# Three SwiGLUs of a decoder trunk: gate and up with the activations stationary and 512 weight columns moving, turned back by 32x32 blocks and on-chip transfers

## The chip, the cores and the metric

The kernel runs on one core of a Trainium2 chip. Its engines are TensorE (PE, matmuls; its weight loads are listed as PEld), VectorE (DVE), ScalarE (ACT), GpSimd (POOL) and the sync engine (SP), which here issues most transfers. The metric is device time in microseconds (us), the median of several runs. One execution is also taken by the hardware profiler; what is quoted as rows below comes from that one.

## The reference

A trunk of two layers over 256 tokens of width 1024, all in fp32. Each layer is a half-step SwiGLU, a token mixer (block-sparse attention in the first layer, latent attention in the second), and another half-step SwiGLU; each of these is preceded by an RMS norm and a shift and scale from the condition `c`, and added back with a gate from `c`. The part that the change touches:

```python
def swiglu(h, w_gate, w_up, w_down):      # D_MODEL = 1024, D_FF = 2816
    return (jax.nn.silu(h @ w_gate) * (h @ w_up)) @ w_down
```

There are four of these: two in each layer.

## The kernel before

**Precision.** Every fp32 operand is split into a high half and a low half in a 32-bit format that TensorE takes at full rate. ACT writes the high half (`hi`, L690) and DVE the low half (`lo`, L691). A product is three matmuls, high by high, high by low and low by high (`mm3`, L897 to L900).

**Weights.** They stream in the order in which they are used, 1 MB at a time, by SP's queue into `raw` (three buffers), and are split into `hi` and `lo` pieces of 128x1024 (eight buffers of each). A weight transfer (L838) waits until a `raw` buffer is free, which is when DVE's `lo` has read it.

**A SwiGLU.** Tokens are two tiles of 128 (`t`), the width 1024 is eight contraction tiles (`k`), and D_FF is 22 blocks of 128 (`f`). The first SwiGLU has a method of its own and is untouched. In the other three, the first four f-blocks (512 columns) are computed with `h` stationary and the weight columns moving: 48 matmuls of 512 columns per token tile, tokens on partitions. ACT takes the Silu (L1077), DVE the product (L1078), and PE turns the result by four 128x128 transposes (L1083) so that f lies on partitions, as the down projection needs it. The other 18 f-blocks are computed with a weight block stationary and `h` moving, so that f lies on partitions at once: for gate and up, eight matmuls of 512 columns (high and low half of `h` side by side, L1112) and eight of 256 (L1120). Here ACT copies one half of the sums (L1124), DVE adds the other (L1125); for every two f-blocks come one Silu (L1127), one product (L1128) and one split into `gh` and `gl` (L913, L914). These halves, called gT, are the stationary side of the down projection, in two halves of 512 output columns; its matmuls are the same `mm3`, with `gh` and `gl` in the place of `h`.

**Buffers.** The accumulators `mm` are a ring of four PSUM banks. `sums` is a pool with two buffers of each tile. `ry` has one buffer.

**Other work.** DVE also reduces the columns of the conditioning weights (`adaw`, L705 and L746) whenever there is room. For each sub-layer a row of gates is written to memory and read back over all partitions on POOL's queue (`gate_d<-grow`, L766, then `gate<-gate_d`, L754).

**Order.** The instructions are not run as written. A planner (`Order`) gives each instruction a cost (`duration`), simulates the engines, and fixes the order on every engine; a wait at the head of an engine's row holds what stands behind it.

Of the kernel before, what the change touches and what calls it, by code (L numbers as in the profile page):

```python
# [63 lines left out]
T_WAIT = 5.6  # L64
TQ_WAIT = 5.4
# [7 lines left out]
G_WAIT = 2.6  # L73
# [22 lines left out]
def weight_tiles():  # L96


    for layer in range(2):
        for idx in range(2):  # L100
            wg, wu, wd = (("ffn_w_" + n, (layer, idx)) for n in ("gate", "up", "down"))
            if (layer, idx) != (0, 0):
                for w in (wg, wu):
                    for k0 in range(0, KD, 4):
                        yield [(*w, 0)], k0, 4, FB
            for f0 in range(FB if (layer, idx) != (0, 0) else B1 * P, F, S):
                for w in (wg, wu):
                    yield [(*w, f0)], 0, KD, min(S, F - f0)
# [26 lines left out]
def lay_out(v):  # L135
# [8 lines left out]
    def rows(k0, j, cols, n, at, c, width=None, step=1, first=0):  # L144
        k = step * j + first if width else k0 + j
        return v[n][at][k * P:(k + 1) * P, c:c + (width or cols)]
# [73 lines left out]
def duration(i, aps):  # L220
# [19 lines left out]
    if e == "DVE":  # L240
# [5 lines left out]
        elif kind == "InstTensorCopy":  # L246
            d = 150.0 + (1.045 if psum else 0.53) * n
        elif kind == "InstMemset":
# [18 lines left out]
class Order:  # L267
# [128 lines left out]
    def place(self, need, nudge={}):  # L396
# [80 lines left out]
        while placed < n:  # L477
# [29 lines left out]
            if self.dma[k]:  # L507
# [3 lines left out]
                dur = dma_free + 850.0 - t  # L511
                if t < HELD and elements(self.aps[k][-1]) * self.aps[k][-1].ap[0][1] <= D:
                    dur = LONE
                if e != "Pool":
# [61 lines left out]
def trunk(ctx: ExitStack, tc: tile.TileContext, a: dict, out: bass.AP):  # L576
# [252 lines left out]
    def wload():  # L829
# [4 lines left out]
        widths = [p[3] for p in parts] if not cols else [cols * len(parts)]  # L834
# [200 lines left out]
    def ffn(layer, idx, h, after, ada_to, start=None, early=None):  # L1035

        last = (layer, idx) == (1, 1)
        with ExitStack() as st:
# [24 lines left out]
            accs = {t: [] for t in range(NT)}  # L1063
            parts = [[], []]
            for t in range(0 if start else NT):
                for i, pl in enumerate(parts):
                    ps = mm_tile()
                    for k in range(KD):
                        if len(pl) <= k:
                            pl += nextw()  # L1070
                        mm3(ps, *hk(h[t], k), *pl[k], start=k == 0, stop=k == KD - 1)
                        if last and not last_ffn:
                            last_ffn.append(nc.cur_bb.bb.instructions[-1].name)
                    accs[t].append(ps)
                acc = accs.pop(t)
                g = sumsp.tile([P, 1024], F32, tag="both", name=nm("g"))[:, :FB]
                nc.scalar.activation(g, acc[0], AF.Silu)  # L1077
# [864 lines left out]
```

## Time and profile before

| what | value |
|---|---|
| median of 3 runs | 976.93 us (976.6 to 978.33) |
| the profiled execution | 976.26 us |
| its span on the core | 974.0 us |
| instructions on PE, DVE, ACT, POOL | 5494, 1392, 1083, 136 |
| bytes moved | 268.29 MB, 275 GB/s |

The span is what the engine rows cover; the rest of the execution's time lies around it. Shares of busy time are averages over the whole program. A wait at one place is seen only in the stretch in which it lies.

### The profile page before, as it was taken

How to read it: one execution, taken by the hardware profiler on the slowest of the kernel's cores; microseconds unless marked ns; L12 is line 12 of the kernel's file. 1: busy time of each engine (PE TensorE's matmuls, PEld its weight loads, DVE VectorE, ACT ScalarE, POOL GpSimd, SP SyncE). 2: the span in 40 equal slices, each digit the busy share in tenths (PEclk: the TensorE clock that was granted, in tenths of full speed). 3: DMA queues.
4: the chain of work that ended last, by engine and by line, in shares of the span. 5: the costliest groups of instructions: out<-in, count | busy, mean ns of one | idle time of the engine just before them, and what ended most of it. 6: DMA issues, size and time to landing. Idle time of an engine off the chain costs nothing.

```text
span 974.0 us, 15044 instructions
## 1 busy us (share of the span) xinstructions
PE 966.2 (99%) x5494; PEld 827.3 (85%) x5494; DVE 828.5 (85%) x1392; ACT 594.1 (61%) x1083; POOL 87.4 (9%) x136
## 2 busy tenths in 40 slices
PE   8999999999999999999999999999999999999998
PEld 7998888888887888888888888888998888888887
DVE  7999999799999999998696699988998798566643
ACT  5689654378666956555377556543689595665521
POOL 2021100022130000000010000000143000000000
PEclk9999999999999999999999999999999999999999
DMA  9988889899877899999786599996553377545630
GB/s 357 408 345 286 323 321 365 302 356 344 322 272 248 291 352 347 328 335 335 280 318 244 203 313 360 349 393 218 196 167 118 131 261 277 197 173 195 237 130 22
DMA packets 56097, 268.29 MB, mean 275 GB/s; under 512 B 6734, under 2 KB 7960, under 8 KB 38104
## 3 DMA queue, kind: packets, MB, share of 16 engines
q1 hardware_dynamic: 53232, 259.23, 72.1%
q0 software_dynamic: 2352, 7.77, 2.6%
q8 instruction: 43, 0.70, 0.3%
q10 hardware_dynamic: 440, 0.34, 0.2%
q14 instruction: 30, 0.25, 0.1%
HBM read 263.09 MB, written 4.23 MB: 274 GB/s over the span
## 4 chain that ended last, share of the span: by engine, by line
PE 97%; DVE 2%; issue 0%; DMA 0%; POOL 0%; ACT 0%; DVEq 0%
PE mm L1112 25%; PE mm L898 16%; PE mm L900 16%; PE mm L899 16%; PE mm L1120 13%; PE at L1198 1%; PE at L1245 1%; PE at L1271 1%; PE tr L948 1%; DVE lo L691 1%; PE tr L1693 1%; PE mm L1884 1%; PE mm L1883 1%; PE mm L1885 1%; DVE adaw L705 1%; PE tr L1393 1%
## 5 line engine op out<-in xcount | busy, mean ns | idle before, releaser
L691 DVE TENSOR_TENSOR lo<-raw,hi 128x1024 fp32r<-128x1024 f32 (+2 forms) x302 | 360.1, 1212 | 78.7 <-ACT hi L690 69.2
L690 ACT ACTIVATE hi<-raw 128x1024 fp32r<-128x1024 f32 (+2 forms) x302 | 307.4, 1045 | 141.4 <-PE mm L900 98.8
L1112 PE MATMUL mm<-h,hi 128*128 128x512 f32 x1104 | 266.2, 392 | 1.3 <-DVE both L1125 1.1
L1112 PEld LDWEIGHTS mm<-h,hi 128*128 128x128 f32 x1104 | 202.3, 188 | 41.0 <-DVE both L1125 1.6
L1120 PEld LDWEIGHTS mm<-h,lo 128*128 128x128 f32 x1104 | 142.7, 191 | 5.8
L1120 PE MATMUL mm<-h,lo 128*128 128x256 f32 x1104 | 146.3, 283 | 0.0
L705 DVE CUSTOM_DVE_ANT_0 adaw<-adaw,c_b,cols 128x1024 f32<-128x1024 f32 (+1 forms) x112 | 140.0, 1268 | 2.1 <-DMA adaw<-in_ada_dram 2.1
L899 PE MATMUL mm<-lo,gh 128*128 128x512 f32 (+1 forms) x356 | 138.0, 388 | 0.0
L898 PE MATMUL mm<-hi,gh 128*128 128x512 f32 (+1 forms) x356 | 138.0, 388 | 0.0
L900 PE MATMUL mm<-hi,gl 128*128 128x512 f32 (+1 forms) x356 | 137.7, 387 | 0.0
L898 PE MATMUL mm<-hi,h 128*128 128x512 f32 (+2 forms) x256 | 99.3, 391 | 0.0
L899 PE MATMUL mm<-lo,h 128*128 128x512 f32 (+2 forms) x256 | 97.8, 385 | 0.0
L900 PE MATMUL mm<-hi,h 128*128 128x512 f32 (+2 forms) x256 | 97.6, 386 | 0.0
L900 PEld LDWEIGHTS mm<-hi,gl 128*128 128x128 f32 x356 | 66.9, 188 | 13.5
L899 PEld LDWEIGHTS mm<-lo,gh 128*128 128x128 f32 x356 | 66.9, 188 | 13.2
L898 PEld LDWEIGHTS mm<-hi,gh 128*128 128x128 f32 x356 | 66.8, 188 | 13.1
L1124 ACT ACTIVATE both<-mm 128x256 f32<-128x256 f32 x108 | 39.8, 376 | 39.6 <-PE mm L1120 38.2
L746 DVE CUSTOM_DVE_ANT_0 adaw<-adaw,c_b,cols 128x1024 f32<-128x1024 f32 x48 | 60.9, 1286 | 0.0
L898 PEld LDWEIGHTS mm<-hi,h 128*128 128x128 f32 x256 | 48.1, 188 | 9.2 <-issue 1.2
L900 PEld LDWEIGHTS mm<-hi,h 128*128 128x128 f32 x256 | 48.1, 188 | 9.1 <-DVE h L914 0.6
L899 PEld LDWEIGHTS mm<-lo,h 128*128 128x128 f32 x256 | 48.1, 188 | 7.8
L913 ACT ACTIVATE gh<-both 128x512 fp32r<-128x512 f32 x27 | 17.0, 631 | 60.8 <-DVE both L1128 60.8
(271 smaller groups left out, 1173.1 us busy)
## 6 DMA issues: line engine op xcount, KB each, us to landing
raw<-in_w_dram SPq DMA_DIRECT2D x140, 1024.0 KB, 6.1
adaw<-in_ada_dram SPq DMA_DIRECT2D x158, 512.0 KB, 6.0
raw<-in_w_dram SPq DMA_DIRECT2D x14, 512.0 KB, 4.1
raw<-in_first_dram SPq DMA_DIRECT2D x7, 512.0 KB, 9.8
raw<-in_first_dram SPq DMA_DIRECT2D x9, 384.0 KB, 9.6
gate<-gate_d POOLq DMA_DIRECT2D x6, 512.0 KB, 8.4
bg<-bias_d POOLq DMA_DIRECT2D x4, 768.0 KB, 6.5
adaw<-in_lat_dram SPq DMA_DIRECT2D x6, 512.0 KB, 6.6
```

Of the source, the lines that this page charges most:

```text
L690: nc.scalar.activation(hi, src, AF.Copy)
L691: nc.vector.tensor_tensor(lo, src, hi.bitcast(F32), op=ALU.subtract)
L705: nc.vector.tensor_tensor_reduce(wt[:, cs], wt[:, cs], c_b[:, cs], 1.0, at, op0=ALU.mult, op1=ALU.add, accum_out=m_cols[:, i, c:c + 1])
L746: nc.vector.tensor_tensor_reduce(wt, wt, c_b, 1.0, places["gates"][:, c:c + 1], op0=ALU.mult, op1=ALU.add, accum_out=g_cols[:, row, k:k + 1])
L898: nc.tensor.matmul(ps, lh, rh, start=start, stop=False)
L899: nc.tensor.matmul(ps, lh, rl, start=False, stop=False)
L900: nc.tensor.matmul(ps, ll, rh, start=False, stop=stop)
L913: nc.scalar.activation(hi, ps, AF.Copy)
L948: nc.tensor.transpose(kslice(pt, j), kslice(y, j), ident)
L1112: nc.tensor.matmul(ps, wh, hk_both(h, k).rearrange("p i t q -> p (i t q)"), start=k == 0, stop=False)
L1120: nc.tensor.matmul(ps[:, S:], wl, hk_both(h, k)[:, 0].rearrange("p t q -> p (t q)"), start=False, stop=k == KD - 1)
L1124: nc.scalar.activation(sums, ps[:, S:], AF.Copy)
```

## The change

In the second, third and fourth SwiGLU all of gate and up is computed with `h` stationary. D_FF is cut into five blocks of 512 and one of 256 columns; in the last one gate and up lie side by side in 512 moving columns. So 24 matmuls of 512 (8 k, 3 products) take the place of 16 of 512 and 16 of 256 for every 128 columns of f. ACT's Silu and DVE's product are done once per block and token tile, with the tokens on partitions.

The result is turned without PE: DVE transposes each 32x32 block inside `g` (`nc.vector.transpose`, into `z`, which takes the single buffer named `ry`), and four transfers on POOL's queue move the 32-partition groups of `z` into the 128 partitions of `w` (two buffers), 64 KB each, or 32 KB for the last block. `gh` and `gl` are then split from `w` (L921, L922 in the changed kernel). The weight columns are permuted on the host to suit. There are 36 such block transposes and 144 transfers. The planner gets a cost for the new transpose and the new transfers. Lines of the changed kernel stand some eight higher: `mm3` is L906 to L908, the low half L699.

```diff
-            for t in range(0 if start else NT):
-                for i, pl in enumerate(parts):
-                    ps = mm_tile()
...
-                def fin(t=t, g=g):
-                    pt = tr_tile()
-                    for j in range(FB // P):
-                        nc.tensor.transpose(kslice(pt, j), kslice(g, j), ident)
-                    pe(FB // P * 0.11)
-                    gh, gl = [gp.tile([P, FB], F32R, tag=f"{nme}_{t}", name=nm(nme)) for nme in ("gh", "gl")]
-                    split_evac(gh, gl, pt)
...
+            def turned(t, f0, n, g):
+                nb = n // P
+                z = tp.tile([P, 512], F32, tag="ry", name=nm("z"), bufs=1)[:, :n].rearrange("p (j m b) -> p j m b", j=4, b=NB)
+                w = sumsp.tile([P, 512], F32, tag="w", name=nm("w"))[:, :n].rearrange("p (i m b) -> p i m b", i=4, b=NB)
+                nc.vector.transpose(z.rearrange("p j m b -> p (j m b)"), g[:, :n])
+                for i in range(4):
+                    nc.gpsimd.dma_start(w[:, i].rearrange("p m b -> p (m b)"),
+                                       z[i * NB:(i + 1) * NB].rearrange("a j m b -> a (j m b)"))
+                gh, gl = [gq.tile([P, nb, P], F32R, tag=f"{nme}{f0 // P}_{t}", name=nm(nme)) for nme in ("gh", "gl")]
+                split_evac(*[x.rearrange("p m (i b) -> p i m b", b=NB) for x in (gh, gl)], w)
+                for j in range(nb):
+                    gT[f0 // P + j, t] = gh[:, j], gl[:, j]
...
+                def mms(t, i, k):
...
+                    mm3(accs[t][i], *hk(h[t], k), *pl[k], start=k == 0, stop=k == KD - 1)
...
+                def side_done(t, i):
+                    if not i:
+                        g[t] = sumsp.tile([P, 512], F32, tag="g", name=nm("g"))
+                        nc.scalar.activation(g[t][:, :n], accs[t][0][:, :n], AF.Silu)
+                    if i == len(sides) - 1:
+                        nc.vector.tensor_tensor(g[t][:, :n], accs[t][i][:, -n:], g[t][:, :n], op=ALU.mult)
+                        turned(t, f0, n, g[t])
...
-            for f0 in range(B1 * P if start else FB, F, S):
+            for f0 in range(B1 * P if start else F, F, S):
```

PE in the second SwiGLU, past its first 512 columns. `mm` are accumulators, `hi` and `lo` weight pieces, `h` the activations. Before:

```order
L1112 MATMUL mm_862_4575<-h_689_3735,hi_836_4421 128x512 x4
L1112 MATMUL mm_862_4575<-h_689_3735,hi_838_4425 128x512 x4
L1112 MATMUL mm_863_4576<-h_689_3735,hi_852_4518 128x512 x4
L1112 MATMUL mm_863_4576<-h_689_3735,hi_854_4522 128x512 x4
L1120 MATMUL mm_862_4575<-h_689_3735,lo_837_4422 128x256 x4
L1120 MATMUL mm_862_4575<-h_689_3735,lo_839_4426 128x256 x4
L1120 MATMUL mm_863_4576<-h_689_3735,lo_853_4519 128x256 x4
L1120 MATMUL mm_863_4576<-h_689_3735,lo_855_4523 128x256 x4
```

These 32 matmuls are one f-block. In the same SwiGLU of the changed kernel the rows read so (`mm_891` is one token tile, `mm_893` the other):

```order
L906 MATMUL mm_891_4631<-hi_875_4566,h_689_3735 128x512
L907 MATMUL mm_891_4631<-lo_876_4567,h_689_3735 128x512
L908 MATMUL mm_891_4631<-hi_875_4566,h_689_3735 128x512
L906 MATMUL mm_893_4639<-hi_875_4566,h_689_3735 128x512
L907 MATMUL mm_893_4639<-lo_876_4567,h_689_3735 128x512
L908 MATMUL mm_893_4639<-hi_875_4566,h_689_3735 128x512
```

All are 512 wide, and the stationary side is a 128x128 piece of `h`; which half it is the names don't tell.

DVE at the end of the last SwiGLU, in the changed kernel: from the transpose of the last block's first token tile on (`z_1952`, `z_1957` are the two token tiles of the 256-wide block; `w_1936` belongs to the block before, `w_1953` and `w_1958` to the last; `L699` are low halves of weights of the down projection):

```order
L1075 STREAM_TRANSPOSE z_1952_9244<-g_1951_9241 128x256
L699 TENSOR_TENSOR lo_1985_9410<-raw_1983_9407,hi_1984_9409 128x1024
L922 TENSOR_TENSOR gl_1938_9168<-w_1936_9161,gh_1937_9167 128x4x4x32
L699 TENSOR_TENSOR lo_1988_9440<-raw_1986_9437,hi_1987_9439 128x1024
L699 TENSOR_TENSOR lo_1990_9444<-raw_1986_9437,hi_1989_9443 128x1024
L699 TENSOR_TENSOR lo_1997_9472<-raw_1995_9469,hi_1996_9471 128x1024
L1075 STREAM_TRANSPOSE z_1957_9258<-g_1956_9255 128x256
L922 TENSOR_TENSOR gl_1955_9252<-w_1953_9245,gh_1954_9251 128x4x2x32
L699 TENSOR_TENSOR lo_1999_9476<-raw_1995_9469,hi_1998_9475 128x1024
L699 TENSOR_TENSOR lo_2002_9494<-raw_2000_9491,hi_2001_9493 128x1024
L699 TENSOR_TENSOR lo_2004_9498<-raw_2000_9491,hi_2003_9497 128x1024
L922 TENSOR_TENSOR gl_1960_9266<-w_1958_9259,gh_1959_9265 128x4x2x32
```

Before, there was no transpose in DVE's row here; its last split of the SwiGLU followed one product, four rows after the last two adds. POOL's row over the same stretch of the changed kernel, where `gate_d` and `gate` are the two transfers of the gate:

```order
L1077 DMA w_1897_8983<-z_1896_8982 128x1x128 x4
L774 DMA gate_d_129<-grow_1916_9066 8x128
L762 DMA gate_1913_9048<-gate_d_129 128x1024
L1077 DMA w_1932_9149<-z_1931_9148 128x1x128 x4
L1077 DMA w_1936_9161<-z_1935_9160 128x1x128 x4
L1077 DMA w_1953_9245<-z_1952_9244 128x1x64 x4
L1077 DMA w_1958_9259<-z_1957_9258 128x1x64 x4
```

The gate's two transfers were alone in this row before; now they stand ahead of the last sixteen moves. PE in the down projection of the last SwiGLU of the changed kernel, where it first reads the last token tile's halves (`gh_1959`), 126 matmuls after that projection began:

```order
L908 MATMUL mm_1961_9269<-hi_1984_9409,gl_1955_9252 128x512
L906 MATMUL mm_1961_9269<-hi_1984_9409,gh_1954_9251 128x512
L907 MATMUL mm_1961_9269<-lo_1985_9410,gh_1954_9251 128x512
L906 MATMUL mm_1993_9467<-hi_1987_9439,gh_1782_8400 128x512
L906 MATMUL mm_1962_9270<-hi_1984_9409,gh_1959_9265 128x512
L907 MATMUL mm_1962_9270<-lo_1985_9410,gh_1959_9265 128x512
L908 MATMUL mm_1962_9270<-hi_1984_9409,gl_1960_9266 128x512
```

The rows for `gh_1954` and `gh_1959` stand at the end of the first half of the outputs, where the last f-blocks stood before as well; between them the second half (`mm_1993`) has begun.

## Rows read from the trace of the kernel before

**Rows 1.** The page's totals: busy time, share of the span and instructions of each engine.

```profile
PE 966.2 (99%) x5494; PEld 827.3 (85%) x5494; DVE 828.5 (85%) x1392; ACT 594.1 (61%) x1083; POOL 87.4 (9%) x136
```

**Rows 2.** The chain of work that ended last, as shares of the span by engine.

```profile
PE 97%; DVE 2%; issue 0%; DMA 0%; POOL 0%; ACT 0%; DVEq 0%
```

**Rows 3.** Windows: length in us, then busy time (and instructions) of PE, PEld, DVE, ACT and POOL, PE's granted clock as a share of full speed, the DMA engines' busy share, and GB/s. The opening; the second SwiGLU (340 to 380); the third (600); the fourth (820 and 880).

```profile
0.00:20.00 20.00, 17.10 (x90) 13.32 (x91) 15.25 (x33) 9.40 (x17) 5.75 (x28) 0.91 0.92 346
340.00:360.00 20.00, 20.00 (x115) 17.43 (x114) 17.94 (x24) 10.74 (x17) 1.16 (x2) 1.00 0.93 338
360.00:380.00 20.00, 20.00 (x114) 17.50 (x113) 19.58 (x31) 11.57 (x17) 0.00 (x0) 1.00 0.96 359
600.00:620.00 20.00, 18.88 (x108) 16.15 (x107) 20.00 (x32) 11.60 (x19) 1.09 (x2) 1.00 0.94 353
820.00:840.00 20.00, 20.00 (x116) 17.68 (x116) 14.35 (x20) 10.46 (x19) 0.00 (x0) 1.00 0.54 199
880.00:900.00 20.00, 20.00 (x120) 17.79 (x119) 12.21 (x18) 12.88 (x21) 1.14 (x2) 1.00 0.61 231
```

**Rows 4.** The chain in order of time in the second SwiGLU: start in us, length in us, what. The two kinds of rows alternate from the first to the last shown.

```profile
353.98 3.65 PE mm L1112 x16
357.63 1.91 PE mm L1120 x16
359.55 3.65 PE mm L1112 x16
...
431.91 3.20 PE mm L1112 x14
```

**Rows 5.** PE's timeline in the first 512 columns of the fourth SwiGLU: start in us, length in us (modelled), engine, line, operation, tiles. Around one group of transposes, and then the first and the last of 23 matmuls in a row.

```profile
801.50 0.40 PE L898 MATMUL mm<-hi,h 128*128 128x512 f32 x1
801.73 0.60 PE L1083 MATMUL tr<-ident,g 128*128 128x128 f32 x4
802.09 0.47 PE L898 MATMUL mm<-hi,h 128*128 128x512 f32 x1
802.40 0.39 PE L899 MATMUL mm<-lo,h 128*128 128x512 f32 x1
...
804.25 0.39 PE L899 MATMUL mm<-lo,h 128*128 128x512 f32 x1
...
809.24 0.39 PE L900 MATMUL mm<-hi,h 128*128 128x512 f32 x1
```

**Rows 6.** The same view in the fourth SwiGLU's down projection: the first and the last of 27 matmuls in a row.

```profile
919.76 0.39 PE L898 MATMUL mm<-hi,gh 128*128 128x512 f32 x1
...
925.65 0.39 PE L900 MATMUL mm<-hi,gl 128*128 128x512 f32 x1
```

**Rows 7.** Groups of instructions by line: engine, operation, out<-in, shapes, count, then busy us, mean ns of one, and the idle time of the engine before them and what ended it. `both` is the tile of the three SwiGLUs in question; `ry` is that of the first SwiGLU, 256 wide.

```profile
L691 DVE TENSOR_TENSOR lo<-raw,hi 128x1024 fp32r<-128x1024 f32 (+2 forms) x302 | 360.1, 1212 | 78.7 <-ACT hi L690 69.2 <-PE mm L1120 6.5 <-issue 2.1
L1125 DVE TENSOR_TENSOR both<-both,mm 128x256 f32<-128x256 f32 x108 | 43.1, 414 | 3.1 <-ACT both L1124 3.0
L1124 ACT ACTIVATE both<-mm 128x256 f32<-128x256 f32 x108 | 39.8, 376 | 39.6 <-PE mm L1120 38.2
L914 DVE TENSOR_TENSOR gl<-both,gh 128x512 fp32r<-128x512 f32 x27 | 18.5, 686 | 6.3 <-ACT gh L913 6.3
L1128 DVE TENSOR_TENSOR both<-both 128x512 f32<-128x512 f32 x27 | 18.4, 683 | 0.1
L930 DVE CUSTOM_DVE_ANT_0 ry<-x,ssq 128x512 f32<-128x512 f32 x10 | 7.5, 749 | 0.1
L1128 DVE TENSOR_TENSOR ry<-ry 128x256 f32<-128x256 f32 x15 | 7.4, 491 | 0.0
L914 DVE TENSOR_TENSOR gl<-ry,gh 128x256 fp32r<-128x256 f32 x15 | 6.2, 416 | 1.0 <-ACT gh L913 1.0
L1078 DVE TENSOR_TENSOR g<-mm,g 128x512 f32<-128x512 f32 x6 | 4.1, 688 | 0.6 <-PE mm L900 0.6
```

**Rows 8.** The same view, PE's 512-wide matmuls of the old form, with PE's idle time before them.

```profile
L1112 PE MATMUL mm<-h,hi 128*128 128x512 f32 x1104 | 266.2, 392 | 1.3 <-DVE both L1125 1.1
```

**Rows 9.** The page's transfers: tiles, queue, count, size of one, median us from issue to landing.

```profile
blat<-gate_d POOLq DMA_DIRECT2D x1, 384.0 KB, 5.4
gate_d<-grow POOLq DMA_DIRECT2D x8, 4.0 KB, 5.5
```

**Rows 10.** Two lines of the kernel by themselves: for L766 the time that one issue takes on POOL (least, median, most, in ns) and its transfers' time to landing (least, median, most, in us); for L754 the latter, its transfers are of 512 KB.

```profile
L766 POOL DMA_DIRECT2D gate_d<-grow x9: 522/566/719, 128.2 to 881.6; - x9
DMA to landing us min/median/max: 1.5/5.3/5.9
...
DMA to landing us min/median/max: 4.0/8.4/11.2
```

**Rows 11.** POOL's timeline in the second and in the fourth SwiGLU: start, length, issue, and in brackets POOL's idle time ahead of it and what ended that.

```profile
349.70 0.57 POOL L766 DMA_DIRECT2D gate_d<-grow  x1 [25.43 <-ACT grow L765]
355.26 0.58 POOL L754 DMA_DIRECT2D gate<-gate_d  x1 [4.99 <-DMA gate_d<-grow]
...
881.58 0.58 POOL L766 DMA_DIRECT2D gate_d<-grow  x1 [90.40 <-ACT grow L765]
886.55 0.56 POOL L754 DMA_DIRECT2D gate<-gate_d  x1 [4.39 <-DMA gate_d<-grow]
```

**Rows 12.** What SP's queue waited for before it issued: line, releaser, us in total, times, longest us. L838 loads weights.

```profile
SPq L838 <- DVE lo L691: 442.8, 132, 15.8
```

More of the change, by code (lines that the diff above doesn't have):

```diff
@@ L102, in weight_tiles @@
             if (layer, idx) != (0, 0):
[L103 to L108, printed above, removed]
+                for f0 in range(0, F, FB):
+                    n = min(FB, F - f0)
+                    for ws in ((wg,), (wu,)) if n == FB else ((wg, wu),):
+                        for k0 in range(0, KD, 4):
+                            yield [(*w, f0, n, 1, 0, n // P) for w in ws], k0, 4, n
+            else:
+                for f0 in range(B1 * P, F, S):
+                    for w in (wg, wu):
+                        yield [(*w, f0)], 0, KD, min(S, F - f0)
             for half in range(2):
@@ L142, in tiled, with rows @@
         return w.reshape(kt, P, -1).transpose(1, 0, 2).reshape(-1)
-    def rows(k0, j, cols, n, at, c, width=None, step=1, first=0):
-        k = step * j + first if width else k0 + j
-        return v[n][at][k * P:(k + 1) * P, c:c + (width or cols)]
+    def rows(k0, j, cols, n, at, c, width=None, step=1, first=0, blocks=0):
+        k = step * j + first if width and not blocks else k0 + j
+        x = v[n][at][k * P:(k + 1) * P, c:c + (width or cols)]
+        return x.reshape(P, blocks, NB, 4).transpose(0, 3, 1, 2).reshape(P, -1) if blocks else x
     out = {"w": np.concatenate([
@@ L833, in wload @@
         kfirst = k0
-        widths = [p[3] for p in parts] if not cols else [cols * len(parts)]
+        widths = [cols * len(parts)] if cols else [p[3] for p in parts]
         cols = sum(widths)
@@ L1090, in ffn @@
-            for f0 in range(B1 * P if start else FB, F, S):
-                if f0 == (SIDE_TO if start else SPLIT_AT):
-                    while start and next(side[0], "end") != "end":
+            def turned(t, f0, n, g):
[10 more added lines that the diff above has]
+                    gT[f0 // P + j, t] = gh[:, j], gl[:, j]
@@ L1093, in ffn @@
+            for f0 in range(B1 * P if start else F, F, S):
+                if f0 == SIDE_TO:
+                    while next(side[0], "end") != "end":
                         bias_step()
                     gq = st.enter_context(tc.tile_pool(name=nm("gp"), bufs=1))
-                if start and f0 == ROPE_AT:
+                if f0 == ROPE_AT:
                     hold(rope_tables)
@@ L1114, in ffn @@
                             pe(0.227)
-                            if start and k in HOOKS and f0 < SIDE_TO:
+                            if k in HOOKS and f0 < SIDE_TO:
                                 bias_step()
```

60 lines of the change are left out of this document (32 added, 28 removed).

## The prediction

> **What bounds the kernel now.** I read the engine totals first: TensorE (PE) is busy 966.2 of 974.0 us, VectorE (DVE) 85%, ScalarE (ACT) 61% [rows 1]. The chain that ended last lies 97% on PE [rows 2], and the windows show PE idle by 0.00 us in most stretches: 1.12 us at 600 to 620, 2.90 us in the opening [rows 3]. So a change is worth what it takes from PE's own row of work, less any wait it puts there. DVE is the engine that could make one: 19.58 and 20.00 of 20 us busy inside the second and third SwiGLU, but only 14.35 in the last [rows 3]. A median of the runs is 976.93, the profiled run 976.26, its span 974.0: sums below are differences, put on the median, which stands 2.93 us above the span.
>
> **Matmuls, the main term.** Between 353.98 and 431.91 fourteen f-blocks of 128 follow each other without a gap: 77.93 / 14 = 5.566 us each, as 16 matmuls of 512 columns (3.65 us, 228 ns each) and 16 of 256 (1.91 us, 119.4 ns) [rows 4]. The same block becomes 24 matmuls of 512 with h stationary. Columns are equal, 12288; eight instructions fewer. The new form already runs in this kernel, in the first block of each of the three SwiGLUs: from 804.25 to 809.24 are 22 starts, 4.99 / 22 = 226.8 ns [rows 5]; the down projection, same shape, gives 5.89 / 26 = 226.5 [rows 6]. So 24 x 226.8 = 5.443 us, saving 0.123 per block, 54 blocks (18 in each of three): 6.6 us. With 226.5 it is 7.0. As lower end I take the 228 ns of the 512-wide half [rows 4]: 5.475 us, 4.9 us in all. I take 6.6.
>
> A pair of 256 costs 239 ns here, 12 more than one 512. The Trainium skill, "TensorE: Matmul & The Clock Gate", section "Wait — 56ns, not 53.3ns?", puts a warm matmul at N / 2.4 GHz plus about 2.5 ns. By that rule a block would go from 16 x (215.8 + 109.2) = 5.200 us to 24 x 215.8 = 5.179, an estimate of 1.1 us in all. The rows, 226.8 and 119.4 ns, disagree with it.
>
> **Transposes on PE.** Six groups of four go. Around one, the second matmul after it starts 802.40 - 801.50 = 0.90 us after the last one before, where two intervals are 0.45: a group costs 0.45 us [rows 5], six of them 2.7 us. Bounds: 0.36 (801.73 to 802.09) to 0.60 each, 2.2 to 3.6.
>
> **Work of ACT and DVE.** Per SwiGLU, DVE now does 36 adds of 414 ns, 9 products of 683, 9 splits of 686, and in the first block 2 products of 688 and 2 such splits [rows 7]: 30.0 us. After it are 10 products and 10 splits of 128x512, two each of 128x256 (at most 491 and 416 ns [rows 7]): 15.5 us, and 12 block transposes. No row shows these. From below no 128x512 fp32 operation is under 0.68, from above I take the 1.21 of a 128x1024 one; nearest is the one-source 128x512 row, 0.75 [rows 7] (0.49 for 256), so 8.5 us, sum 24.0, and 29.2 at the upper end. DVE gets lighter by 6 us or 1. A strided write of the low half is not in the rows either; at 1.21 for each of ten it takes 5 us of that back. ACT loses 36 copies of 376 ns and gains nothing. All this lies under PE. The 1.12 us of 600 to 620 came where PE waited for DVE adds that go (L1125, 1.1 us [rows 8]); I take 1.1 back and charge 0.6 for new evictions that meet a full DVE at the same place: 0.5.
>
> **The moves.** Each block and token sends z to w by four transfers of the POOL queue, hidden as long as gT is wanted later than it arrives. One issue costs 566 ns (median) [rows 10]. An on-chip transfer is in no row. Nearest by size and start are the 4 KB ones off the same queue, 5.5 us to landing; 384 KB took 5.4 [rows 9]. The bounds are 1.5, the least of the 4 KB, and 11.2, the most of 512 KB [rows 10]. With 5.5, m, from a transpose's end to its four transfers landed, is 3 x 0.566 + 5.5 = 7.2 us (3.2 to 12.9).
>
> z has one buffer, so the next transpose waits m, and on DVE the splits behind it wait too. Inside a SwiGLU two transposes come per 96 matmuls, 21.8 us, against 2 x (7.2 + 0.75) = 15.9: covered up to m = 10.1. The close place is the end. Call D0 the start of the down projection. The products of the last 512-wide block can run when PE has 48 matmuls (10.9 us) left before D0; two of them (1.4 us) later the first transpose starts, at D0 - 9.4 and ends at D0 - 8.65. Then four times m, three more transposes (0.75, 0.49, 0.49) and a split of 0.41: the last gT stands at D0 + 4m - 6.5, with 7.2 at 22.3 us. PE first wants it after 126 rows of the down projection, 126 x 0.2266 = 28.6 us. So 6.3 us are spare, and the chain shows on PE above m = 8.8 (landing 7.1), then 4 us for each us of m in each SwiGLU. The queue order puts gate's two transfers ahead of the last w transfers on POOL; the second waits some 5 us for the first [rows 11], which shifts this chain once, within the spare. Splits of weights queued behind the waiting transposes wait m less the 5 to 8 us of DVE work between: 2.5 us at most, in buffers that hold eight tiles. So I cost the moves at nothing; without that cover each us is 12 us in all.
>
> **Sum.** 6.6 + 2.7 + 0.5 = 9.8 off: span 964.2, time **967.1**.
>
> **Rivals.**
>
> *The moves land late (slower).* Place: the end of each SwiGLU, m above 8.8. With the 8.4 us of the 512 KB gate reads off the same queue [rows 10], m is 10.1: 4 x 1.3 = 5.2 us per SwiGLU, 15.6 in three, 982.7; only in the two with full DMA engines (0.96 and 0.94 share, against 0.54 in the last [rows 3]) 977.5. The gain is gone at m = 9.6. Against it: 4 KB transfers landed in 5.56 us (349.70 to 355.26) and 4.97 us (881.58 to 886.55), at DMA shares of 0.93 and 0.61 [rows 3, 11], so load adds little to a small transfer. For it: 144 of them, four queued at once, in 512-byte runs. A mild form, m about 9.1, costs 3.6: 970.7.
>
> The Trainium skill, "SBUF — State Buffer", section "🔬 SBUF: two separate sides", speaks against the change: GpSimd cannot write the descriptors of its queue's transfers while DVE runs a two-port operation, and the next section gives 620 ns alone against some 3100 overlapped. Where DVE was busy 17.94 of 20 us a 4 KB transfer took 5.56 us, where it was busy 12.21, 4.97: the trace shows 0.6, not 2.5 [rows 3, 11]. Estimated from the page, 2.5 us more per round would put m at 9.7, about no gain.
>
> *The added traffic slows the weight stream.* 8.2 MB more move over the DMA engines (30 x 256 + 6 x 128 KB), about 2.8 in each SwiGLU; at 353 to 359 GB/s [rows 3] some 8 us in each of the two that are full, if the stream set the pace: about 983. Against it: transfers wait for buffers, not the reverse; SP waits 442.8 us for DVE's low halves before a weight load [rows 12].
>
> *The matmul pace doesn't move.* If the longer run of the new form went at 5.566 / 24 = 231.9 ns, only the transposes and 0.5 are left: 973.7. No steady row shows that pace.
>
> **How the numbers follow.** Forecast as summed 0.60; mild tail wait (969 to 974) 0.17; pace unmoved 0.05; moves late 0.11; stream slowed 0.07. The forecast's own ends: 4.9 + 2.2 - 0.5 gives 970.3, 7.0 + 3.6 + 1.1 gives 965.2. To leave out no more than 2 in 10 the range goes through the mild wait and the unmoved pace to 974.5, below to 964.8. A measurement tells 0.2%, 1.95 us, from no change. All of the first three cases are faster, 0.82; the late moves and the stream are split, 0.06 within it and 0.12 slower.
>
> **What would show it.** After: f-blocks of the second to fourth SwiGLU at 5.44 us in the chain, starts 226.8 ns apart; DVE busy less by 3 to 18 us, ACT by 40; move landings about 5.5 us; PE idle under 0.3 us at the three starts of the down projection. The forecast is wrong if there the chain steps from PE to DMA (w from z) and the transpose, or if windows inside those SwiGLUs show PE waiting for low halves of weights.

## The result and the profile after

The changed kernel takes 966.6 us (median of 4 runs, 965.64 to 967.55), the kernel before, timed beside it, 976.76. The ratio is 0.9894, 95% interval 0.9876 to 0.9911: 10.2 us less, by the interval 8.7 to 12.1. The forecast was 967.1 (964.8 to 974.5). The profiled execution of the changed kernel has a span of 963.9 us.

The page's totals and the chain by engine, as in [rows 1] and [rows 2]:

```profile
PE 957.4 (99%) x5034; PEld 803.2 (83%) x5038; DVE 816.1 (85%) x1326; ACT 563.8 (58%) x981; POOL 165.2 (17%) x280
...
PE 98%; DMA 0%; ACT 0%; DVE 0%; POOL 0%; issue 0%; ACTq 0%
```

Of the 10.1 us between the two spans, 8.8 are work that PE no longer does (966.2 to 957.4) and 1.3 are time in which PE stands still (7.8 to 6.5). The kernel is still a row of matmuls; what became lighter beside it, DVE by 12.4 us and ACT by 30.3, shows only as far as PE had waited for it. POOL got 77.8 us more, its 144 issues.

Windows at four of the places of [rows 3] (length, busy time of PE, PEld, DVE, ACT, POOL, granted clock, DMA share, GB/s):

```profile
0.00:20.00 20.00, 17.84 (x87) 13.66 (x88) 15.05 (x33) 9.42 (x17) 5.75 (x28) 1.00 0.93 344
360.00:380.00 20.00, 20.00 (x90) 16.57 (x89) 17.69 (x23) 11.29 (x14) 4.32 (x8) 1.00 0.97 372
600.00:620.00 20.00, 20.00 (x90) 16.48 (x89) 18.05 (x24) 9.32 (x12) 5.41 (x10) 1.00 0.98 357
820.00:840.00 20.00, 20.00 (x90) 16.57 (x89) 13.05 (x14) 9.48 (x11) 4.32 (x8) 1.00 0.68 215
```

The 1.12 us in which PE stood still at 600 to 620 are gone. In 20 us PE now runs 90 matmuls where it ran 114 shorter and longer ones. The opening, which the change does not touch, has 0.74 us less idle time, at a granted clock of 1.00 against 0.91; three more executions of the changed kernel had spans of 964.9 to 965.9, so this execution is a short one.

PE's timeline in the fourth SwiGLU, between two interruptions by other work (start, length, line, tiles):

```profile
790.24 0.39 PE L907 MATMUL mm<-lo,h 128*128 128x512 f32 x1
...
877.30 0.39 PE L908 MATMUL mm<-hi,h 128*128 128x512 f32 x1
```

These are the first and the last of 385 matmuls in a row: 87.06 / 384 = 226.7 ns from start to start, so an f-block of 24 takes 5.441 us, against 5.566 in [rows 4]. The new form keeps over 87 us the pace that [rows 5] showed over 5.

The new operations, by line: duration in ns (least, median, most), then for the moves the issue's duration on POOL and the time to landing in us:

```profile
L1075 DVE STREAM_TRANSPOSE z<-g x36: 435/703/712, 343.1 to 918.9; 128x512 f32<-128x512 f32 x30, 128x256 f32<-128x256 f32 x6
  DMA w<-z: 2.1, 3
...
L1077 POOL DMA_DIRECT2D w<-z x144: 535/562/597, 344.5 to 921.5; - x144
  ACT gh L921: 10.5, 11
DMA to landing us min/median/max: 1.7/5.2/7.2
```

A block transpose of 512 columns takes 0.70 us, one of 256 0.44. The time m from a transpose's end to the landing of its last move is 7.3 us by the median of the 36 rounds, worked out from the trace's landings (5.0 to 9.3; by SwiGLU 7.5, 7.9 and 7.3). DVE waited 2.1 us in all for z to be free and ACT 10.5 us for moves to land. What PE itself waited for, in the whole program (total us, times, longest):

```profile
PE tr L1819 <- DVE zeros L1767: 1.3, 1, 1.3
PE tr L1851 <- ACT diag L1841: 0.9, 1, 0.9
PE mm L906 <- ACT h L921: 0.5, 1, 0.5
```

None of these is a move or a block transpose.

### The profile page after: what moved, and what is told of

The parts are those of the page before. It is cut to its first block, busy times and chain, and to the rows that moved or that the text cites. A ratio compares the mean times of both kernels' runs of the same rounds, so it can differ in the third digit from the quotient of the medians.

```text
span 963.9 us, 14341 instructions
## 1 busy us (share of the span) xinstructions
PE 957.4 (99%) x5034; PEld 803.2 (83%) x5038; DVE 816.1 (85%) x1326; ACT 563.8 (58%) x981; POOL 165.2 (17%) x280
## 3 DMA queue, kind: packets, MB, share of 16 engines
q0 software_dynamic: 6960, 16.43, 5.0%
## 4 chain that ended last, share of the span: by engine, by line
PE 98%; DMA 0%; ACT 0%; DVE 0%; POOL 0%; issue 0%; ACTq 0%
PE mm L906 26%; PE mm L907 26%; PE mm L908 26%; PE mm L1135 6%; PE mm L1143 3%; PE at L1220 1%; PE at L1267 1%; PE at L1293 1%; PE tr L1715 1%; PE mm L1906 1%; PE tr L956 1%; PE mm L1905 1%; PE mm L1907 1%; PE tr L1415 1%; PE tr L1905 1%; PE at L1228 1%
## 5 line engine op out<-in xcount | busy, mean ns | idle before, releaser
L699 DVE TENSOR_TENSOR lo<-raw,hi 128x1024 fp32r<-128x1024 f32 (+2 forms) x302 | 360.5, 1211 | 92.4 <-ACT hi L698 91.4
L906 PE MATMUL mm<-hi,h 128*128 128x512 f32 (+2 forms) x688 | 266.8, 390 | 0.5 <-ACT h L921 0.5
L907 PE MATMUL mm<-lo,h 128*128 128x512 f32 (+2 forms) x688 | 266.3, 388 | 0.0
L908 PE MATMUL mm<-hi,h 128*128 128x512 f32 (+2 forms) x688 | 265.5, 387 | 0.0
L906 PEld LDWEIGHTS mm<-hi,h 128*128 128x128 f32 x688 | 129.1, 188 | 27.5 <-issue 1.2
L908 PEld LDWEIGHTS mm<-hi,h 128*128 128x128 f32 x688 | 129.2, 188 | 25.6 <-DVE h L922 0.2
L907 PEld LDWEIGHTS mm<-lo,h 128*128 128x128 f32 x688 | 129.2, 188 | 25.0 <-DVE lo L699 0.4
L906 PE MATMUL mm<-hi,gh 128*128 128x512 f32 (+1 forms) x356 | 137.7, 389 | 0.0
L908 PE MATMUL mm<-hi,gl 128*128 128x512 f32 (+1 forms) x356 | 137.2, 387 | 0.0
L1077 POOL DMA_DIRECT2D w<-z x144 | 77.9, 561 | 290.9 <-issue 115.9
L908 PEld LDWEIGHTS mm<-hi,gl 128*128 128x128 f32 x356 | 66.9, 188 | 13.7
L906 PEld LDWEIGHTS mm<-hi,gh 128*128 128x128 f32 x356 | 66.9, 188 | 13.3
L754 DVE CUSTOM_DVE_ANT_0 adaw<-adaw,c_b,cols 128x1024 f32<-128x1024 f32 x48 | 61.0, 1285 | 0.3 <-DMA adaw<-in_ada_dram 0.3
L1135 PE MATMUL mm<-h,hi 128*128 128x512 f32 x240 | 58.1, 392 | 0.0
L1332 POOL TENSOR_TENSOR hr<-hv,mhalf 128x4 f32<-128x4 f32 (+1 forms) x24 | 40.4, 1685 | 63.9 <-DVE hv L1331 61.2
L1135 PEld LDWEIGHTS mm<-h,hi 128*128 128x128 f32 x240 | 43.9, 188 | 8.6 <-DVE ry L1148 0.2
L943 POOL TENSOR_TENSOR rstd<-ssq,mhalf 128x1 f32<-128x1 f32 x12 | 11.4, 947 | 197.3 <-DVE ssq L938 195.3
L1105 ACT ACTIVATE g<-mm 128x512 f32<-128x512 f32 (+1 forms) x36 | 19.9, 553 | 24.6 <-PE mm L908 22.9
```

The source lines that it names most:

```text
L699: nc.vector.tensor_tensor(lo, src, hi.bitcast(F32), op=ALU.subtract)
L754: nc.vector.tensor_tensor_reduce(wt, wt, c_b, 1.0, places["gates"][:, c:c + 1], op0=ALU.mult, op1=ALU.add, accum_out=g_cols[:, row, k:k + 1])
L906: nc.tensor.matmul(ps, lh, rh, start=start, stop=False)
L907: nc.tensor.matmul(ps, lh, rl, start=False, stop=False)
L908: nc.tensor.matmul(ps, ll, rh, start=False, stop=stop)
L1077: nc.gpsimd.dma_start(w[:, i].rearrange("p m b -> p (m b)"), z[i * NB:(i + 1) * NB].rearrange("a j m b -> a (j m b)"))
```

## The experiments

The theory: the gain is 6.6 us of matmul starts that PE no longer makes, 2.7 us of transposes, and a stall; the moves are free because a round of four lands before the next one needs `z`, and would cost from m = 8.8 us on. The rivals: the moves take part of the gain back; the pace is not a matter of the number of matmuls; the queue or the added traffic matters. The planner fixes the order of every engine's row anew for each of these kernels, by its own costs, so a run shows its edit together with the order that follows from it.

**No turning.** In `turned` the transpose and the transfers are left out, and the halves are split from `g` as it lies:

```diff
-                nc.vector.transpose(z.rearrange("p j m b -> p (j m b)"), g[:, :n])
-                for i in range(4):
-                    nc.gpsimd.dma_start(w[:, i].rearrange("p m b -> p (m b)"),
-                                       z[i * NB:(i + 1) * NB].rearrange("a j m b -> a (j m b)"))
...
-                split_evac(*[x.rearrange("p m (i b) -> p i m b", b=NB) for x in (gh, gl)], w)
+                split_evac(*[x.rearrange("p m (i b) -> p i m b", b=NB) for x in (gh, gl)],
+                           g[:, :n].rearrange("p (i m b) -> p i m b", i=4, b=NB))
```

> The changed kernel without any turning: no block transposes and no transfers, the halves are split from the product as it lies (so the down projection gets unturned data). The theory that the moves lie wholly under PE's work expects 966.6, within 0.7 us. If the chain of moves at the ends of the three SwiGLUs, or the added traffic, still costs something, this kernel is faster by that: 1 to 4 us. DVE would be busy some 24 us less, POOL some 78.

Measured 966.78 us (966.42 to 966.92), ratio to before 0.9898 [0.9882, 0.9915]. Its page:

```profile
PE 957.5 (99%) x5038; PEld 803.6 (83%) x5038; DVE 797.7 (83%) x1290; ACT 565.1 (59%) x981; POOL 84.8 (9%) x136
```

PE is busy as long as in the changed kernel, DVE 18 us less (24 were expected), POOL 80. Thirty-six transposes, 144 transfers and 8.7 MB (POOL's queue moves 16.43 MB with them, 7.77 without) cost nothing that can be measured. That settles the rival of the added traffic too.

**Low halves in two.** The extra matmuls are put back, and nothing else; there are 528 of them, where the change took away 8 in each of 54 f-blocks, 432, because the first 512 columns are split here too:

```diff
-                    mm3(accs[t][i], *hk(h[t], k), *pl[k], start=k == 0, stop=k == KD - 1)
+                    ps, (lh, ll), (rh, rl) = accs[t][i], hk(h[t], k), pl[k]
+                    nc.tensor.matmul(ps, lh, rh, start=k == 0, stop=False)
+                    nc.tensor.matmul(ps, lh, rl, start=False, stop=False)
+                    for c in (slice(0, 256), slice(256, 512)):
+                        nc.tensor.matmul(ps[:, c], ll, rh[:, c], start=False, stop=k == KD - 1 and c.start > 0)
+                    pe(3 * 512 * 0.422e-3)
```

> The changed kernel, with the low-by-high product of gate and up (the third of three) done as two matmuls of 256 columns in place of one of 512: 528 pairs. The theory that the main gain is a fixed price for each matmul, seen before as 2 x 119.4 ns against 226.8, expects 528 x 12.0 ns = 6.3 us more: 972.9. With the 2.5 ns for each matmul of the Trainium skill (TensorE: Matmul & The Clock Gate) it would be 528 x 2.6 ns = 1.4 us, an estimate: 968.0. If the gain came from ACT and DVE doing less, not from PE's instructions: 966.6.

Measured 975.28 us, ratio 0.9986 [0.9977, 0.9996]: 8.7 us more than the changed kernel, most of the gain gone. PE's timeline in the fourth SwiGLU, where L1099 is the first matmul of each three:

```profile
860.13 0.40 PE L1099 MATMUL mm<-hi,h 128*128 128x512 f32 x1
860.37 0.39 PE L1100 MATMUL mm<-lo,h 128*128 128x512 f32 x1
860.60 0.40 PE L1102 MATMUL mm<-hi,h 128*128 128x256 f32 x2
...
873.37 0.40 PE L1099 MATMUL mm<-hi,h 128*128 128x512 f32 x1
```

From 860.13 to 873.37 are 19 groups, 696.8 ns each; three matmuls of 512 took 3 x 226.7 = 680.1. A split costs 16.7 ns, 528 of them 8.8 us, as measured, and not 12.0; 432 of them would be 7.2 us. So the main term is the number of matmuls, at the same columns, the same bytes and the same work on DVE and ACT. The 2.6 ns a pair, an estimate from the 2.5 ns of the Trainium skill (TensorE: Matmul & The Clock Gate, "Wait — 56ns, not 53.3ns?"), are not what this form shows. Whether the price belongs to the second start or to the second weight load that each matmul here brings along, no run tells apart.

**The old kernel without its PE transposes.** In the kernel before, the first block's halves are split from `g` directly:

```diff
-                    pt = tr_tile()
-                    for j in range(FB // P):
-                        nc.tensor.transpose(kslice(pt, j), kslice(g, j), ident)
-                    pe(FB // P * 0.11)
...
-                    split_evac(gh, gl, pt)
+                    split_evac(gh, gl, g)
```

> The kernel before without its 24 PE transposes (the halves of the first 512 columns are split from the product unturned, read from SBUF and not from PSUM). At 0.45 us for each group of four: 2.7 us less, 974.1. If the gaps around the transposes were really those of the evictions beside them, less than 1 us: 976. The 1.1 us in which PE waits for DVE in the third SwiGLU should stay.

Measured 973.59 us (972.45 to 974.93), ratio 0.9968 [0.9956, 0.998]: 2.0 to 4.3 us less than before. Its totals, and the window at the old stall:

```profile
PE 964.2 (99%) x5470; PEld 825.3 (85%) x5470; DVE 829.5 (85%) x1392; ACT 595.3 (61%) x1083; POOL 84.2 (9%) x136
...
600.00:620.00 20.00, 20.00 (x117) 17.54 (x116) 18.70 (x30) 11.45 (x18) 1.09 (x2) 1.00 0.91 348
```

PE no longer stands still there, although all the adds that it had waited for [rows 8] are still in the program, and although the stall was expected to stay. So the adds alone do not make it; that it hung on the order of DVE's row, which is another one here, is likely but not shown. Of 3.1 us between the spans (974.0 and 970.9) 2.0 are work of PE (966.2 to 964.2), which would be 0.33 us for a group of transposes. PE's rows say otherwise: in the kernel before, each of the six groups takes 0.45 us from start to start, as in [rows 5]. Totals of two programs with different orders do not resolve this 0.7 us. The other 1.1 is idle time.

**PE transposes in the new form.** The moves are replaced by the way of the old first block; the weight columns stay permuted, so f comes out in another order:

```diff
-                nc.vector.transpose(z.rearrange("p j m b -> p (j m b)"), g[:, :n])
-                for i in range(4):
-                    nc.gpsimd.dma_start(w[:, i].rearrange("p m b -> p (m b)"),
-                                       z[i * NB:(i + 1) * NB].rearrange("a j m b -> a (j m b)"))
+                pt = tr_tile()
+                for j in range(nb):
+                    nc.tensor.transpose(kslice(pt, j), kslice(g, j), ident)
+                pe(nb * 0.11)
...
-                split_evac(*[x.rearrange("p m (i b) -> p i m b", b=NB) for x in (gh, gl)], w)
+                split_evac(*[x.rearrange("p m q -> p (m q)") for x in (gh, gl)], pt[:, :n])
```

> The changed kernel, but its results are turned by 128x128 transposes on PE, as the old first block did it, in place of the 32x32 blocks and the transfers. 132 transposes, as 30 groups of four and 6 of two. If a group of four costs PE 0.45 us and the transfers cost nothing now: 33 x 0.45 = 14.9 us more than the changed kernel's 966.6, so 981.5, slower than before by 0.5%. If the transfers have a hidden price of some us, the result is lower by that; if transposes are cheaper when they stand between the new matmuls (0.36 us a group), 978.5.

Measured 986.93 us, ratio 1.0103 [1.0088, 1.0118], 20.3 more than the changed kernel and slower than before. PE's rows around one group, its one long wait, and the window behind that (columns as in [rows 3]):

```profile
819.92 0.62 PE L906 MATMUL mm<-hi,h 128*128 128x512 f32 x2
820.38 0.60 PE L1075 MATMUL tr<-ident,g 128*128 128x128 f32 x4
820.73 0.48 PE L907 MATMUL mm<-lo,h 128*128 128x512 f32 x1
821.05 0.39 PE L908 MATMUL mm<-hi,h 128*128 128x512 f32 x1
...
579.58 0.66 PE L1075 MATMUL tr<-ident,g 128*128 128x128 f32 x4 [3.68 <-DVE g L1105]
...
580.00:600.00 20.00, 20.00 (x86) 16.46 (x84) 15.57 (x20) 8.65 (x10) 0.00 (x0) 0.91 0.94 350
```

The second of the two L906 starts at about 820.15, so a group takes 0.90 - 0.45 = 0.45 us, as in [rows 5]; 33 of them give the 14.9 us expected. But the span grew by 21.2 us, to 985.1. PE's idle time makes 4.3 of that (6.5 to 10.8), 3.68 of it at one transpose that stood in PE's row ahead of its product. PE's busy time rose by 16.9 us (957.4 to 974.3), 2.0 more than the transposes; part of it is the granted clock, 0.91 in the 20 us behind that wait and 0.50 from 581.4 to 583.6. So 981.5 was missed by 5.4 us, with the price of a group right. This is the part of the change on which the sign hangs: h stationary without a way around PE would have been slower.

**Every round of moves twice.**

```diff
-                for i in range(4):
+                for i in (0, 1, 2, 3, 0, 1, 2, 3):
```

> The changed kernel with every round of four moves issued twice over (eight transfers, the same bytes to the same place), so that a round lands 4 x 0.56 = 2.2 us later and the moved bytes double. By the prediction's chain m becomes 7.2 + 2.3 = 9.5, 0.7 over the point of 8.8, and four times that in each of three SwiGLUs is 8.4 us: 975.0. By what the changed kernel's trace shows, transposes at the end of a SwiGLU stand 8.0 to 11 us apart because DVE's row is paced by the weight splits between them, so that most of a longer m would vanish in those gaps: 966.6 to 969. If added traffic slows the weight stream, 8.4 MB more would show in the second and third SwiGLU alone: up to 16 us.

Measured 1058.48 us, ratio 1.0836: a miss on all three counts. The edit did more than was meant. POOL's timeline at the end of the second SwiGLU, and what POOL waited for in all:

```profile
470.84 0.54 POOL L1077 DMA_DIRECT2D w<-z  x1 [7.96 <-DVE z L1075]
...
475.91 0.54 POOL L1077 DMA_DIRECT2D w<-z  x1 [1.25 <-DMA w<-z]
...
479.85 1.20 POOL L1077 DMA_DIRECT2D w<-z  x2 [0.39 <-issue]
...
  DMA w<-z: 102.6, 58
```

PE's two largest waits in the whole program:

```profile
PE mm L906 <- ACT gh L921: 29.9, 6, 9.1
PE mm L906 <- ACT g L1105: 17.1, 5, 3.9
```

The second four write where the first four write, so each waits for the first to land: m is not 2.2 us longer but becomes two landings. The last issue ends 10.2 us after the first began, and has then still to land. Two such rounds are no longer under the 21.8 us of a block: PE's idle time grew to 70.4 us (span 1054.9, busy 984.5). The wait for `gh` is that at the end of a SwiGLU, the wait for `g` mostly that in its middle: with m at 12.5 us by the median (up to 16.1) both places cost, and the end more. PE's busy time grew by another 27.1 us, most of it matmuls at a lower granted clock (0.85 from 470 to 560). The run shows how steep the far side is, not where it begins.

**Three times:** the same with twelve transfers.

> The same with twelve transfers a round: 4.5 us later than in the changed kernel, three times the bytes. By the chain m is 11.7, 2.9 over the point, 11.7 us in each SwiGLU, 35 in three: about 1002, and two rounds in a SwiGLU's middle, 2 x (11.7 + 0.7) = 24.8, no longer fit into the 21.8 us of a block. With the gaps of 8 to 11 us only about 1 to 3 us a round are left to wait for, four rounds in three SwiGLUs, less the spare of the last: 972 to 990.

Measured 1182.9 us, ratio 1.2098, missed for the same reason, three landings to a round: 206 us over before, and again 124 over the kernel with two.

**A round later by one, two and four operations of GpSimd.** This asks the same question without the wait of a transfer for another. A select that keeps every value of z stands between transpose and moves:

```diff
                 nc.vector.transpose(z.rearrange("p j m b -> p (j m b)"), g[:, :n])
+                for _ in range(1):                  # 2, 4
+                    nc.gpsimd.affine_select(z[:, 0, 0], z[:, 0, 0], pattern=[[0, NB]], compare_op=ALU.is_ge,
+                                            fill=0.0, base=0, channel_multiplier=0)
```

> The changed kernel with one operation of GpSimd between each block transpose and its four moves: a select over 32 columns of z that keeps every value. Such an operation took 1.24 us where the kernel already has it, so m, read as about 7.1 us in the second and third SwiGLU of the changed kernel and 5.1 in the last, becomes 8.4 and 6.4. Both are under the prediction's point of 8.8: 966.6, within 1.5 us. If the cover is really smaller than the prediction worked out, 970 or more.

> The same with two such operations: m about 9.6 in the second and third SwiGLU, 7.6 in the last. By the prediction's slope (4 us for each us above 8.8) 0.8 x 4 in two SwiGLUs, 6.4 us: 973. If the gaps that DVE's row already has between the transposes take it up: 966.6 to 968.

> The same with four: m about 12.1 and 10.1. By the end of the SwiGLU alone 3.3 x 4 in two and 1.3 x 4 in the last, 31.6 us: 998. If every round of a SwiGLU counts, because two rounds (2 x 12.8 us) no longer fit under a block's 21.8, then up to 3.8 us more for each of the blocks between: about 1010 to 1030.

Measured 967.24 us (966.61 to 967.8) with one, as expected; 966.23 (966.08 to 967.12) with two, so not the 973 of the slope; 977.5 (973.8 to 982.85) with four, a miss of all figures given, and the whole gain lost (ratio 1.0012). The select took not 1.24 us but 0.21 to 1.27. By the median m was 8.4, 8.5 and 7.4 us in the three SwiGLUs with one, 9.3, 9.4 and 6.3 with two, 10.5, 10.5 and 8.2 with four. With two, the end of the third SwiGLU on DVE:

```profile
636.30 0.45 DVE L1075 STREAM_TRANSPOSE z<-g 128x256 f32<-128x256 f32 x1 [1.58 <-issue]
646.31 0.45 DVE L1075 STREAM_TRANSPOSE z<-g 128x256 f32<-128x256 f32 x1 [0.70 <-DMA w<-z]
```

The second of these starts when the moves of the first have landed: from 636.75 to 646.31, m = 9.6, and PE loses nothing there. Over the last four rounds of the second SwiGLU m is 9.6 on average, too. There the down projection's first matmul (D0) and the last `gl` read so:

```profile
440.71 0.39 PE L906 MATMUL mm<-hi,gh 128*128 128x512 f32 x1
...
477.58 0.42 DVE L922 TENSOR_TENSOR gl<-w,gh 128x256 fp32r<-128x256 f32 x1 [2.46 <-ACT gh L921]
```

The last `gl` is ready 37.3 us after D0, long after the 28.6 of the forecast, and PE has no wait for it. With four, the first stretch in which PE loses time (DVE, then PE; this execution took 973.8 us, the shortest of ten):

```profile
408.02 0.71 DVE L1075 STREAM_TRANSPOSE z<-g 128x512 f32<-128x512 f32 x1 [4.00 <-DMA w<-z]
418.63 0.71 DVE L1075 STREAM_TRANSPOSE z<-g 128x512 f32<-128x512 f32 x1
432.47 0.71 DVE L1075 STREAM_TRANSPOSE z<-g 128x512 f32<-128x512 f32 x1 [4.68 <-DMA w<-z]
...
409.42 0.50 PE L906 MATMUL mm<-hi,h 128*128 128x512 f32 x1 [1.70 <-ACT g L1108]
433.86 0.50 PE L906 MATMUL mm<-hi,h 128*128 128x512 f32 x1 [2.37 <-ACT g L1108]
```

Two rounds take 432.47 - 408.02 = 24.45 us, where the 96 matmuls of a block take 21.8: 2.7 too many, and PE waits 2.37. The way there: the transpose waits 4.68 us for z, the Silu waits for the `g` that a transpose has not yet read, and PE waits for the bank that the Silu has not yet emptied. PE's four waits of this kind are 7.3 us. The 3.7 us from this execution to the median are in no trace.

At the ends PE never waits in these three runs, and the order of its row tells why. By the programs and traces of the four kernels, the last token tile's halves are first read after so many matmuls from D0, and the last `gl` is ready, and its first matmul starts, so many us after D0:

| kernel | second SwiGLU | third | fourth |
|---|---|---|---|
| changed | 145: 30.8, 33.2 | 143: 30.2, 32.8 | 126: 27.3, 29.0 |
| one select | 152: 31.4, 35.5 | 145: 30.4, 33.7 | 134: 30.1, 30.8 |
| two | 172: 37.3, 39.4 | 154: 34.1, 35.3 | 155: 31.9, 35.6 |
| four | 208: 46.8, 48.0 | 204: 46.8, 47.5 | 182: 41.6, 42.2 |

The planner costs each select and puts these matmuls later, among those of the second half of the outputs. So these runs do not hold the order still while m grows: the limit of 8.8 at the end, for the order that the changed kernel has, stays untested. What they show is that with the order planned anew a mean m of 9.6 at the end costs nothing, and that the cover ends first in the middle of a SwiGLU, where the forecast had put its limit at m = 10.1: the two rounds above are 24.45 us where that limit allows 21.8.

**The moves on another queue.** Only the issuing engine changes, `nc.scalar` or `nc.sync` in place of `nc.gpsimd`.

> The changed kernel with the moves issued by ScalarE's queue in place of GpSimd's. If the transfers are hidden where they are, the time stays at 966.6, within 1.5 us, as long as ACT's own waits behind the issues stay short; ACT has 0.5 of its time free. If GpSimd's descriptors were held up by VectorE (the Trainium skill, SBUF - State Buffer, on the two sides), landings would drop from the median of 5.2 us by 1 us or more. If they land as before, that hold-up plays no part here.

Measured 973.83 us (972.01 to 978.59), 7.2 over the changed kernel. The profiled execution took 977.27, so it is one of the longer ones. The landing times, the longest piece of the chain at the end of the second SwiGLU, PE there, and PE at the end of the third:

```profile
DMA to landing us min/median/max: 1.9/4.7/12.3
...
453.33 12.32 DMA w<-z
...
466.44 0.50 PE L906 MATMUL mm<-hi,gh 128*128 128x512 f32 x1 [2.77 <-ACT gh L921]
467.99 0.80 PE L908 MATMUL mm<-hi,gl 128*128 128x512 f32 x1 [0.81 <-DVE gl L922]
469.01 0.63 PE L907 MATMUL mm<-lo,gh 128*128 128x512 f32 x1
469.44 0.63 PE L908 MATMUL mm<-hi,gl 128*128 128x512 f32 x1
...
661.89 0.50 PE L906 MATMUL mm<-hi,gh 128*128 128x512 f32 x1 [1.99 <-ACT gh L921]
```

The median landing is 0.5 us shorter than on POOL's queue, but single transfers take up to 12.3 us, and m is over 10 us in 11 of the 36 rounds, against none in the changed kernel. That is the wait that the forecast's first rival had described, though not at the last `gT`: PE stood 2.77 and 0.81 us for `gh` and `gl` of the last 512-wide block's second token tile, about 100 matmuls after D0, and then ran for a while at 0.43 us a matmul (granted clock 0.50 from 468.6 to 471.1), before it was back at 0.23. At the end of the third SwiGLU it stood 1.99 us.

> The changed kernel with the moves issued by SP's queue, among the weight loads. SP waits 447 us in all for DVE's low halves before it issues a weight load, up to 10.9 us at once; a move behind such a load is late by as much, and weight loads behind a move wait for its transpose. Expected slower than the changed kernel: 970 to 990. If the queue does not matter, 966.6.

Measured 966.74 us, ratio 0.9889 [0.9872, 0.9907]: the same as the changed kernel, a miss. SP's queue waited like this:

```profile
SPq L846 <- DVE lo L699: 290.9, 112, 11.6
SPq L1077 <- DVE z L1075: 52.1, 25, 5.0
```

It spends 52 us waiting for transposes, which delay weight loads, and the waits of weight loads for buffers fall from 447 to 291 us: the loads had that much room. Landings took 4.4 us by the median and 8.5 at most. The rule of the Trainium skill (SBUF — State Buffer, "🔬 SBUF: two separate sides") on GpSimd's descriptors is about two-port operations of DVE; if DVE's operations here were such, the moves should be markedly faster off GpSimd's queue. Medians of 5.2, 4.7 and 4.4 us agree in direction, at 0.5 to 0.8 us, under the 1 us that was asked for. Nor does the queue change the issuing engine alone: the same 144 moves are 4608 packets from POOL's queue and 20736 from ACT's or SP's. So the runs do not show that hold-up. The time is the same from POOL's and SP's queue and 7.2 us longer from ACT's; why transfers land late there is not shown.

## Why the prediction was right

**The matmuls** were forecast at 0.123 us a block and 6.6 in all. The pace after, 226.7 ns, gives 5.566 - 5.441 = 0.125 and 6.7. The size is confirmed by the splitting run in the other direction: 16.7 ns for each matmul that is put back, against 0.125 / 8 = 15.6 ns for each that went. What the forecast made of it, 239 ns for a pair of 256 and 12 over one 512, was too low; the sum did not use it, since it compared whole blocks, in which also the 512-wide half was slower by 1.3 ns a matmul.

**The transposes** were forecast at 2.7 us. PE's rows agree: 0.45 us for each of the six groups before, and the same in the run with 132 transposes. The totals of the run without them give 2.0, if the stall is set apart, just under the forecast's bounds of 2.2 to 3.6. Which of the two holds is open.

**The stall**: 1.1 us was credited and 0.6 charged for new ones. By the totals PE's work fell by 8.8 us, for which 6.7 + 2.0 stand, and its idle time by 1.3, for which 0.5 was forecast: by them the transposes were 0.7 too dear and the idle time 0.8 too small, and the sum of 9.8 came out at 10.1 of span. That these two errors cancel is luck. The reason given for the stall was not borne out: PE had waited for adds which go, but in the old kernel without transposes the adds stayed and the stall went. The new wait that was charged did not come at that place either: PE's one new wait, 0.5 us for ACT's `h` (L921), is at 778.9 us, at the start of the fourth SwiGLU. The opening's 0.74 us less idle time is in no term; the cause of it was not looked for.

**DVE and ACT.** The transpose was costed at 0.75 and 0.49 and took 0.70 and 0.44. DVE's total fell by 12.4 us, 4.1 a SwiGLU, inside the forecast's 1 to 6. ACT fell by 30.3 us, not 40; it is on no path and was not followed up.

**The moves** were costed at nothing, and the run without them says the same to 0.2 us. The landing was taken at 5.5 us and is 5.2; m was taken as 7.2 and is 7.3 by the median. That it fits is in part luck: the forecast left out the 0.55 us from a transpose's end to the first issue (900.58 to 901.14 for the second transpose below). The working of the end of the last SwiGLU was not right in its times. Its transposes, with the down projection's first matmul (D0) and the last split of `gl`:

```profile
900.12 0.39 PE L906 MATMUL mm<-hi,gh 128*128 128x512 f32 x1
...
890.21 0.70 DVE L1075 STREAM_TRANSPOSE z<-g 128x512 f32<-128x512 f32 x1
899.88 0.70 DVE L1075 STREAM_TRANSPOSE z<-g 128x512 f32<-128x512 f32 x1
908.14 0.45 DVE L1075 STREAM_TRANSPOSE z<-g 128x256 f32<-128x256 f32 x1
909.62 1.23 DVE L699 TENSOR_TENSOR lo<-raw,hi 128x1024 fp32r<-128x1024 f32 x1 [1.04 <-ACT hi L698]
...
918.93 0.43 DVE L1075 STREAM_TRANSPOSE z<-g 128x256 f32<-128x256 f32 x1
927.04 0.42 DVE L922 TENSOR_TENSOR gl<-w,gh 128x256 fp32r<-128x256 f32 x1
```

Against D0 the four stand at -9.9, -0.2, 8.0 and 18.8; worked out were -9.4, then -1.45, 6.5 and 14.2. The last `gl` ends at 27.3, 1.2 us before the forecast's 28.6, not 6.3. The landing of the moves spaces only one of them: the third transpose starts 0.1 us after the moves before it have landed, the second 2.3 and the fourth 3.0 us after, because DVE's row has weight splits between them, which wait for ACT's high halves (909.62). So the chain was longer than worked out, and the spare smaller. What the forecast took as fixed, PE's first read after 126 matmuls, is not: it is 126 in the last SwiGLU alone, 145 and 143 in the others, and in a kernel with longer rounds the planner moves it. That is why a mean m of 9.6 still cost nothing at the end of the second SwiGLU. Whether 8.8 would have been the limit with the order held still is open; the limit that the runs with selects met first was the other one that the forecast had named, two rounds in 21.8 us.

**The rivals.** The late moves did not happen here but exist: the kernel with ACT's queue shows them, at landings of up to 12.3 us. The weight stream was not slowed. The pace of the new form was the one read from the first block. The estimate by the 2.5 ns a matmul of the Trainium skill (TensorE: Matmul & The Clock Gate, "Wait — 56ns, not 53.3ns?") would have given 1.1 us for the main term, and the runs give 6.7.

## What to carry to other kernels

Where one engine is busy 99% of the span, count its instructions at equal columns: the kernel's own rows of the new form, measured where that form already runs, gave the gain to 0.1 us. Work that is taken off this engine may take long elsewhere as long as it has a place to wait; before relying on that, work out how long a round may last (here about 10 us against 7), with the single buffer that serializes it, in the middle of the loop as well as at its end, and lengthen it on purpose to see where it starts to cost. Where a planner fixes the orders, compare the orders too: the last read moved from 126 matmuls to 182 as the rounds grew, so a lengthened round did not meet the same schedule. An experiment that repeats a transfer into the same place measures a wait for the first, not a delay.

## What the runs showed of the hardware

A matmul of 512 columns split into two of 256 costs 16.7 ns more, in a row where every matmul has its own weight load. Transfers of 64 KB inside SBUF in runs of 512 bytes land after 5.2 us (1.7 to 7.2) by the median from POOL's queue, 4.7 (up to 12.3) from ACT's and 4.4 (up to 8.5) from SP's, while 215 to 372 GB/s move in all; four queued at once land as one of 4 KB had (5.3, [rows 10]). One such move is 32 packets from POOL's queue and 144 from the other two. A 32x32 block transpose on DVE takes 0.70 us for 128x512, as long as DVE's other fp32 operations of that size (0.68 to 0.75).

PE's clock fell to the lower of its two levels (granted 0.50, 0.43 us a matmul) after 2.77 and 0.81 us in which PE stood still in the kernel with ACT's queue, for 2.6 us (468.58 to 471.14), and there again after 1.99 us (0.51 from 662.5 to 665.8). Stops of 1.3 to 2.4 us in the kernel with four selects left it at 1.00 (433.8 to 438, behind the longest). What decides between the two no run shows.
